# When the operands of the seven products are made in a hybrid decoder layer, and where the second pass's operands and the raw weights stand

## The chip, the cores and the metric

One core of a Trainium2 chip runs the whole layer as one program. The metric is the device time of one execution in microseconds (us), the median of several runs. TensorE (PE in the profile) multiplies into PSUM. VectorE (DVE) and ScalarE (ACT) prepare its operands and empty PSUM. GpSimd (POOL) and SyncE (SP) here mostly issue transfers, each on a queue of its own that goes in order.

## What is computed

A layer runs over 1024 prompt tokens and 8 single decode tokens (T = 1032 columns), all in float32 accuracy. The part that the change touches is the end of the layer: the output projection with its residual, the second norm, and the MLP.

```python
mix = jnp.concatenate([pool_out, rwkv_out], axis=-1) @ w_out     # 1024 x 1024
x = x + mix
h2 = _rmsnorm(x, norm2_g)
x = x + jnp.square(jax.nn.relu(h2 @ w_up)) @ w_down              # 1024 x 4096, 4096 x 1024
y = _rmsnorm(x, norm_f_g)
```

## The kernel before, in words

**Split operands.** Every operand of a large product is split in two parts: a high part `h`, rounded by ACT (`act`, line 94), and a low part `l`, the rest, subtracted by DVE. A product is then three matmuls (h·h, h·l, l·h) for each 128 rows of the contraction (`gemm`, line 185). Weights come from DRAM 128 x 512 at a time. `weights` (lines 159 and 167) and `split` (line 176) put the parts into two rings, `wh` and `wl`, of six tiles each.

**Two passes over the tokens.** Tokens are in channel-major tiles, and everything from the output projection on goes in two halves: 512 columns, then 520 (512 prompt tokens and the 8 decode tokens). `x1[half]` holds the residual stream of a half and is loaded by `load_x1` (line 866).

**Output projection of the second half** (pool `opb`). `mixed` (lines 879 and 881) loads and splits the eight mixer rows. `out_block` (line 885 on) makes one output tile: 21 matmuls of 260 columns into one of two PSUM banks, then one DVE add into `x1` (line 890). Eight output tiles `m`, two column blocks each, take the first seven mixer rows; a second loop of 16 short blocks of 3 matmuls (weights `w7`) adds the eighth row.

**Second norm.** `norm2` squares the residual on ACT, sums over the tiles on DVE (line 921), sums over the partitions by a matmul with ones (line 922), and takes the inverse root (`rstd`, lines 137 to 139).

**The up projection as seven products.** A half's columns are cut in two and the contraction in two, and instead of eight block products seven are made of sums of blocks. `up_operands(half)` makes the seven token operands in high and low parts (names x11, x21, x22, xt1 to xt4, each with h and l), four slices `k` each. A slice `k` takes 15 DVE operations: 4 times norm and gain (line 942), 4 subtractions (line 945), 7 low parts (line 935), and 7 roundings on ACT. `up_pair(p)` makes output tiles 2p and 2p+1: it loads four raw weight blocks a11, a21, a12, a22 on SP's queue (line 974), makes four sums s1 to s4 on DVE in tiles of their own (named `as` in the profile, line 978), splits seven weights, and runs seven products of 12 matmuls (line 991). The outputs are combined (line 1006), squared, and split (line 1002). All raw weights and sums stand in pool `mp`, which is opened after `opb` is closed and lies in its room.

**The down projection.** `downs(G, ms)` yields eight steps for each group `G` of four up tiles: one weight split, 12 matmuls of 512 columns in the first half (24 of 260 in the second), and one or two DVE adds into `x1` (line 1054). `up_pair` takes four such steps between its own products. `G` runs from 0 to 14; pairs 0 to 15 belong to the first half, 16 to 31 to the second, and `G == 7` is the turn: `up_operands(1)` stands there, with four of the eight down steps behind it.

**What sets the order.** The program is written in one order, and a scheduler at compile time puts each engine's instructions into a fixed sequence: of those that it reckons ready, the one written first. On the chip each engine keeps to that sequence and waits where an input is late. A tile can be written again only after its last reader, and a tile in reused room waits for the tiles that stood there.

The end of the out projection before reads:

```python
        load_x1(1)
        norm2(0, 512, lambda x: op.tile([P, 512], F32, tag="n2", name=x, bufs=2))
        up_operands(0)
        for m in range(KT):
            w = weights(I["w_out"][m, :, :(KT - 1) * P])
            for o in (0, 260):
                out_block(m, w, ops, 1, o, 260)
```

## Time and profile before

| What | us |
|---|---|
| median of three runs | 1369.51 |
| lowest and highest of the three | 1365.20, 1369.58 |
| the profiled execution's own time | 1369.36 |
| its span (first to last instruction) | 1367.6 |

The profile is of one execution. Times are us from the start of the span. "Busy" is the time in which an engine executes. "PEclk" or "granted clock" is the TensorE clock in that stretch as a share of full speed: 1.00 is the upper of its two levels, 0.50 the lower. A row such as "PE mx <- DVE x" says which engine waited, with which tile, for whom. A number in square brackets at the end of a row is the idle time of the engine before this instruction, and what ended it.

### The profile page before, as it was taken

To read this page: it belongs to the slowest core of one execution; us is meant where nothing else is said; L and a number is where in the kernel's file an instruction comes from. 1 tells how busy PE (TensorE), PEld (TensorE's weight loads), DVE (VectorE), ACT (ScalarE), POOL (GpSimd) and SP (SyncE) were. 2 spreads that over 40 slices of the span, in tenths; PEclk is the share of its full clock that TensorE was granted. 3 is DMA by queue.
4 is the path that set the end of the run, shared out by engine and by line. 5 is a ranking of instruction groups with operands and counts; after the bars stand their busy time and mean duration, and the time that the engine had idled before them with its cause. 6 is when DMAs were issued, how large, how long until landed. Compare 5 with 4: busy or idle time off the path is not lost.

```text
span 1367.6 us, 26992 instructions
## 1 busy us (share of the span) xinstructions
PE 1277.1 (93%) x10228; PEld 1156.3 (85%) x10228; DVE 1060.8 (78%) x2321; ACT 827.3 (60%) x2004; POOL 88.1 (6%) x178
## 2 busy tenths in 40 slices
PE   5999999999999899958899999999799999999996
PEld 5987888798777767857788989989699999999996
DVE  8887676879777665775887777878989778788775
ACT  7667677766877665533655655546566555455552
POOL 4111001210100211110000000000000000000000
PEclk9999999999999999979899999999899999999998
DMA  6222123322312433512233333332234333333321
GB/s 208 95 55 79 42 58 81 114 75 61 73 43 47 130 136 115 186 56 72 86 108 94 108 102 97 102 101 93 71 100 147 101 94 101 99 95 109 93 63 63
DMA packets 109347, 128.27 MB, mean 94 GB/s; under 512 B 54585, under 2 KB 62905, under 8 KB 109209
## 3 DMA queue, kind: packets, MB, share of 16 engines
q1 hardware_dynamic: 97120, 92.22, 23.1%
q0 software_dynamic: 10240, 32.48, 7.2%
q10 hardware_dynamic: 1856, 1.85, 0.4%
q8 instruction: 80, 1.31, 0.4%
q14 instruction: 51, 0.41, 0.1%
HBM read 113.23 MB, written 13.51 MB: 93 GB/s over the span
## 4 chain that ended last, share of the span: by engine, by line
PE 72%; DVE 12%; ACT 10%; DMA 3%; issue 2%; POOL 1%; SPq 0%; DVEq 0%; ACTq 0%; POOLq 0%
PE dn L185 24%; PE b L991 21%; PE pj L185 10%; PE mx L185 6%; ACT SV L94 2%; PE pcs L608 1%; DVE tm L525 1%; PE sc L431 1%; PE pcs L605 1%; ACT TT L94 1%; PE pcs L601 1%; ACT wh L94 1%; DVE x L1060 1%; DMA a<-in_w_up 1%; PE bkt L445 1%
## 5 line engine op out<-in xcount | busy, mean ns | idle before, releaser
L185 PE MATMUL dn<-uh,wh 128*128 128x260 f32 (+1 forms) x736 | 237.8, 324 | 6.0 <-DVE x L1054 5.4
L185 PE MATMUL dn<-uh,wl 128*128 128x260 f32 (+1 forms) x736 | 237.5, 323 | 2.1 <-DVE wl L167 2.1
L185 PE MATMUL dn<-ul,wh 128*128 128x260 f32 (+1 forms) x736 | 237.3, 323 | 0.1
L94 ACT ACTIVATE wh<-wr 128x512 fp32r<-128x512 f32 x230 | 143.2, 623 | 127.5 <-PE b L991 39.0
L185 PE MATMUL pj<-xh,wh 128*128 128x258 f32 (+3 forms) x576 | 172.7, 300 | 13.9 <-ACT wh L94 13.9
L167 DVE TENSOR_TENSOR wl<-wr,wh 128x512 fp32r<-128x512 f32 x230 | 156.0, 682 | 31.6 <-ACT wh L94 22.5
L185 PE MATMUL pj<-xl,wh 128*128 128x258 f32 (+3 forms) x576 | 170.6, 296 | 0.0
L185 PE MATMUL pj<-xh,wl 128*128 128x258 f32 (+3 forms) x576 | 170.4, 296 | 0.1
L185 PEld LDWEIGHTS dn<-uh,wh 128*128 128x128 f32 x736 | 139.0, 189 | 16.1 <-DVE x L1054 6.0
L1054 DVE TENSOR_TENSOR x<-dn,x 128x260 f32<-128x260 f32 (+1 forms) x192 | 98.7, 514 | 68.0 <-PE dn L185 64.8
L185 PEld LDWEIGHTS dn<-uh,wl 128*128 128x128 f32 x736 | 139.0, 189 | 13.9 <-DVE wl L167 2.8
L185 PEld LDWEIGHTS dn<-ul,wh 128*128 128x128 f32 x736 | 139.1, 189 | 9.3 <-DVE ul L1002 0.4
L94 ACT ACTIVATE wh<-as 128x512 fp32r<-128x512 f32 x128 | 80.1, 628 | 76.5 <-PE dn L185 72.7
L185 PEld LDWEIGHTS pj<-xh,wh 128*128 128x128 f32 x576 | 110.3, 192 | 17.7 <-ACT wh L94 13.9
L94 ACT ACTIVATE wh<-a 128x512 fp32r<-128x512 f32 x96 | 60.5, 632 | 104.1 <-PE dn L185 56.0
L185 PEld LDWEIGHTS pj<-xl,wh 128*128 128x128 f32 x576 | 110.4, 192 | 2.3 <-issue 1.9
L185 PEld LDWEIGHTS pj<-xh,wl 128*128 128x128 f32 x576 | 110.1, 191 | 1.8 <-issue 1.0
L176 DVE TENSOR_TENSOR wl<-as,wh 128x512 fp32r<-128x512 f32 x128 | 87.9, 687 | 4.6
L185 PE MATMUL mx<-mh,wh 128*128 128x260 f32 (+1 forms) x192 | 67.2, 352 | 18.6 <-DVE x L890 18.2
L1002 DVE TENSOR_TENSOR ul<-u,uh 128x256 fp32r<-128x256 f32 (+1 forms) x128 | 54.1, 425 | 21.7 <-ACT uh L94 21.5
L176 DVE TENSOR_TENSOR wl<-a,wh 128x512 fp32r<-128x512 f32 x96 | 65.8, 687 | 4.9 <-ACT wh L94 1.0
L94 ACT ACTIVATE c<-c 128x256 f32<-128x256 f32 (+1 forms) x128 | 53.0, 414 | 21.0 <-DVE c L1006 20.9
(380 smaller groups left out, 3453.4 us busy)
## 6 DMA issues: line engine op xcount, KB each, us to landing
wr<-in_w_down SPq DMA_DIRECT2D x128, 256.0 KB, 2.6
a<-in_w_up SPq DMA_DIRECT2D x128, 256.0 KB, 2.6
wr<-in_w_in POOLq DMA_DIRECT2D x72, 256.0 KB, 3.2
wr<-in_w_out POOLq DMA_DIRECT2D x26, 256.0 KB, 3.3
xr<-in_xT SPq DMA_DIRECT2D x16, 256.0 KB, 3.6
mr<-mix SPq DMA_DIRECT2D x8, 260.0 KB, 3.5
x<-in_xT SPq DMA_DIRECT2D x2, 1040.0 KB, 9.6
blk<-AA SPq DMA_DIRECT2D x16, 128.0 KB, 2.7
```

Source lines behind the costliest of these rows:

```text
L94: A.activation(out, in_, func, bias=bias, scale=scale, **k)
L167: V.tensor_tensor(l[:, :w], raw[:, :w], f32(h[:, :w]), op=ALU.subtract)
L176: V.tensor_tensor(l, raw, f32(h), op=ALU.subtract)
L185: PE.matmul(ps, lhs, rhs, start=i == 0, stop=i == n - 1)
L431: PE.matmul(psc[:, c, :], BK[:, c, 2 * h:2 * h + 2, :], AR[:, c, :, h, :], start=True, stop=True)
L445: PE.transpose(pt[:, c, :], BK[:, c, 2 * h:2 * h + 2, :].rearrange("p a t -> p (a t)"), ident)
L525: V.tensor_tensor(pr[:, q], l[:, q].unsqueeze(2).to_broadcast([64, m, m, m]), r[:, q].rearrange("p k j -> p j k").unsqueeze(1).to_broadcas ...
L601: PE.matmul(pq, AR[:, c, 0, :, :], SV[:, c, :, :], start=True, stop=True)
L605: PE.matmul(pa, TT[:, g, :, :], Q, start=True, stop=True)
L991: PE.matmul(ps, lhs[:, c], rhs, start=k == i == 0, stop=k == 3 and i == 2)
L1002: V.tensor_tensor(ul, u, f32(uh), op=ALU.subtract)
L1054: V.tensor_tensor(d, ps[:, :n], d, op=ALU.add)
```

## The change

- The seven token operands of the first half are made one slice `k` at a time, one slice after every second output tile of the out projection, and not in one run ahead of it. The norm of the first half is made in two blocks of 256 columns in other tiles.
- The norm of the second half moves from between `up_pair(0)` and `up_pair(1)` into `G == 1`.
- The operands of the second half are made a slice each in `G == 2` to `5`, in small tiles `xsh`, `xsl` (two of each), and stored to DRAM tiles `XD` from POOL's queue: 56 stores of 128 x 260. At `G == 7`, 14 loads of 128 x 1040 bring them into the tiles of the first half's operands.
- The raw weights stand in pool `hq`, which is opened before `opb`. Of eight tiles five are left: s1, s2 and s4 are written over a21, a11 and a12. The sums are made behind the split of a12. Load order is a11, a21, a22, a12.
- `load_x1` loads in four pieces of two tiles, not in two of four.

```diff
     def load_x1(half):
-        for k in range(0, KT, 4):
-            SY.dma_start(x1[half][:, k:k + 4, :], I["xT"][:, k:k + 4, c0:c0 + n])
+        for k in range(0, KT, 2):
+            SY.dma_start(x1[half][:, k:k + 2, :], I["xT"][:, k:k + 2, c0:c0 + n])
...
+    XD = {i: [dr.tile([P, 4, 260], F32R, name=f"xd{i}{x}") for x in "hl"] for i in KIND}
+
+    def open_operands(half):
+        for i in KIND:
+            XO[half][i] = [hq.tile([P, 4, 260], F32R, tag=f"x{i}{x}", name=f"x{i}{x}{half}") for x in "hl"]
+            if half:
+                for t, d in zip(XO[half][i], XD[i]):
+                    GP.dma_start(t, d)
+
-    def up_operands(half):
+    def up_operands(half, k):
...
+        def put(i, x):
+            if half:
+                h, l = (mp.tile([P, 260], F32R, tag=f"xs{y}", name=f"xs{i}{y}{k}", bufs=2) for y in "hl")
+            else:
+                h, l = (t[:, k, :q] for t in XO[half][i])
             act(h, x)
             V.tensor_tensor(l, x, f32(h), op=ALU.subtract)
+            if half:
+                for t, d in zip((h, l), XD[i]):
+                    GP.dma_start(d[:, k, :], t)
...
-        a = {}
-        for k in range(2):
-            for f in range(2):
-                i = f"{f + 1}{k + 1}"
-                a[i] = mp.tile([P, 512], F32, tag=f"a{i}", name=f"a{i}_{p}")
-                SY.dma_start(a[i], I["w_up"][f0 + f][:, 512 * k:512 * k + 512])
-        for out, x, y, op in (("s3", "11", "21", ALU.subtract), ("s1", "21", "22", ALU.add), ("s2", "s1", "11", ALU.subtract),
-                              ("s4", "12", "s2", ALU.subtract)):
-            a[out] = mp.tile([P, 512], F32, tag=f"a{out}", name=f"a{out}_{p}")
-            V.tensor_tensor(a[out], a[x], a[y], op=op)
+        a, parts = {}, {}
+        raw = lambda i: hq.tile([P, 512], F32, tag=f"a{i}", name=f"a{i}_{p}")
+        for f, k in ((0, 0), (1, 0), (1, 1), (0, 1)):
+            i = f"{f + 1}{k + 1}"
+            a[i] = raw(i)
+            SY.dma_start(a[i], I["w_up"][f0 + f][:, 512 * k:512 * k + 512])
+
+        def parts_of(s):
+
+            def plus(out, x, y, op, at):
+                a[out] = a[at] if at else raw(out)
+                V.tensor_tensor(a[out], a[x], a[y], op=op)
+
+            if s == "12":
+                parts[s] = split(a[s])
+                plus("s3", "11", "21", ALU.subtract, None)
+                plus("s1", "21", "22", ALU.add, "21")
+                plus("s2", "s1", "11", ALU.subtract, "11")
+                plus("s4", "12", "s2", ALU.subtract, "12")
+                return parts[s]
+            return split(a[s])
...
-        norm2(0, 512, lambda x: op.tile([P, 512], F32, tag="n2", name=x, bufs=2))
-        up_operands(0)
+        for c in (0, 256):
+            norm2(c, 256, lambda x: xtmp(x, 260))
+        open_operands(0)
         for m in range(KT):
             w = weights(I["w_out"][m, :, :(KT - 1) * P])
             for o in (0, 260):
                 out_block(m, w, ops, 1, o, 260)
+            if m % 2:
+                up_operands(0, m // 2)
...
     up_pair(0)
-    for c, n in BLK[1:]:
-        norm2(c, n, tmp)
     up_pair(1)
...
     for G in range(15):
         first, rest = downs(G, range(4)), downs(G, range(4, 8))
+        if G == 1:
+            for c, n in BLK[1:]:
+                norm2(c, n, tmp)
+        if 2 <= G < 6:
+            up_operands(1, G - 2)
         if G == 7:
-            up_operands(1)
+            open_operands(1)
             for _ in first:
                 pass
```

## Rows read from the trace of the kernel before

**Rows 1.** The page's busy time by engine: us, share of the span, instructions.
```profile
PE 1277.1 (93%) x10228; PEld 1156.3 (85%) x10228; DVE 1060.8 (78%) x2321; ACT 827.3 (60%) x2004; POOL 88.1 (6%) x178
```

**Rows 2.** The page's 40 slices, busy tenths of PE, and PE's clock.
```profile
PE   5999999999999899958899999999799999999996
...
PEclk9999999999999999979899999999899999999998
```

**Rows 3.** Busy time by engine in six stretches; then clock, DMA share, GB/s.
```profile
563.30:576.60 13.30, 11.27 (x70) 10.11 (x69) 9.12 (x17) 5.99 (x12) 2.15 (x4) 0.87 0.77 270
576.60:627.60 51.00, 35.38 (x273) 35.17 (x272) 32.14 (x83) 16.88 (x38) 3.66 (x6) 0.83 0.17 50
627.60:637.00 9.40, 8.17 (x48) 6.21 (x47) 6.82 (x17) 0.84 (x2) 0.00 (x0) 1.00 0.00 1
637.00:669.00 32.00, 21.66 (x138) 20.04 (x139) 28.01 (x59) 20.35 (x47) 0.00 (x0) 0.87 0.35 112
789.60:831.80 42.20, 42.20 (x266) 37.93 (x265) 32.72 (x60) 23.33 (x48) 0.00 (x0) 1.00 0.32 102
958.00:990.00 32.00, 25.03 (x118) 20.16 (x117) 29.23 (x72) 17.30 (x45) 0.00 (x0) 0.84 0.21 66
```

**Rows 4.** Waits of PE from 560 to 700 us: total, times, longest.
```profile
PE mx L185 <- DVE x L890: 18.2, 6, 15.6
PE b L991 <- ACT wh L94: 4.1, 2, 3.2
PE ss L922 <- DVE acc L921: 3.2, 1, 3.2
```

**Rows 5.** Waits of PE from 950 to 1000 us, same columns.
```profile
PE dn L185 <- DVE x L1054: 4.1, 1, 4.1
PE dn L185 <- DVE wl L167: 2.1, 1, 2.1
```

**Rows 6.** Timeline of PE, late out projection and the first product: start, us, instruction.
```profile
626.68 0.28 PE L185 MATMUL mx<-mh,wh 128*128 128x260 f32 x1
626.80 0.28 PE L185 MATMUL mx<-ml,wh 128*128 128x260 f32 x1
...
639.90 0.39 PE L991 MATMUL b<-x11h,wh 128*128 128x256 f32 x1 [3.17 <-ACT wh L94]
```

**Rows 7.** Timeline of DVE: residual add, first and last of 60 operand operations.
```profile
571.53 0.43 DVE L890 TENSOR_TENSOR x<-mx,x 128x260 f32<-128x260 f32 x1 [3.17 <-DMA x<-in_xT]
...
576.71 1.66 DVE L942 SCALAR_TENSOR_TENSOR b<-x,vec,rs 128x256 f32<-128x256 f32 x4
...
598.54 0.41 DVE L935 TENSOR_TENSOR xt4l<-b,xt4h 128x256 fp32r<-128x256 f32 x1
```

**Rows 8.** Timeline of SP's queue: first loads of raw up weights.
```profile
636.65 31.68 SPq L974 DMA_DIRECT2D a<-in_w_up  x15
```

**Rows 9.** DVE by kind, 789.6 to 831.8 us: count, busy us, mean ns, idle before.
```profile
L1054 DVE TENSOR_TENSOR x<-dn,x 128x512 f32<-128x512 f32 x8 | 5.5, 692 | 5.2 <-PE dn L185 5.1
L167 DVE TENSOR_TENSOR wl<-wr,wh 128x512 fp32r<-128x512 f32 x8 | 5.5, 686 | 0.3
```

**Rows 10.** ACT by kind, same stretch and columns.
```profile
L94 ACT ACTIVATE wh<-as 128x512 fp32r<-128x512 f32 x8 | 5.0, 629 | 4.7 <-PE dn L185 4.7
L94 ACT ACTIVATE wh<-a 128x512 fp32r<-128x512 f32 x6 | 3.8, 632 | 7.7 <-PE dn L185 4.1 <-PE b L991 3.6
```

**Rows 11.** Timeline at the end of a pair: split of s4, later split of a12.
```profile
833.90 0.68 DVE L176 TENSOR_TENSOR wl<-as,wh 128x512 fp32r<-128x512 f32 x1
...
837.26 0.63 ACT L94 ACTIVATE wh<-a 128x512 fp32r<-128x512 f32 x1 [2.04 <-PE dn L185]
```

**Rows 12.** DVE sums of line 921, whole run: count, shortest, median, longest ns.
```profile
L921 DVE TENSOR_TENSOR acc<-acc,sq x21: 419/429/693, 553.8 to 667.9; 128x260 f32<-128x260 f32 x14, 128x512 f32<-128x512 f32 x7
```

**Rows 13.** The page's DMA issues: KB each, median us from issue to landing.
```profile
a<-in_w_up SPq DMA_DIRECT2D x128, 256.0 KB, 2.6
...
mix<-ys POOLq DMA_DIRECT2D x16, 128.0 KB, 2.2
...
out_yT<-x SPq DMA_DIRECT2D x2, 512.0 KB, 3.1
```

**Rows 14.** Landing of the two 1040 KB loads of x1, 560 to 580 us.
```profile
DMA to landing us min/median/max: 8.0/9.6/11.3
```

More of the change, by code (lines that the diff above doesn't have):

```diff
@@ L927, in up_operands, with normed @@
         c0, n = HALF[half]
         q = n // 2
-        for i in KIND:
-            XO[half][i] = [hq.tile([P, 4, 260], F32R, tag=f"x{i}{x}", name=f"x{i}{x}{half}") for x in "hl"]
-        def put(i, k, x):
-            h, l = (t[:, k, :q] for t in XO[half][i])
+        b = {}
+        def normed(i, kk, o):
+            b[i] = xtmp(f"b{i}_{k}_{half}", q)
+            V.scalar_tensor_tensor(b[i], x1s(kk, o, q), col(V_G2, kk), rs2[:, o:o + q], ALU.mult, ALU.mult)
+        def put(i, x):
[3 more added lines that the diff above has]
+                h, l = (t[:, k, :q] for t in XO[half][i])
@@ L934, in put @@
             act(h, x)
             V.tensor_tensor(l, x, f32(h), op=ALU.subtract)
-        for k in range(4):
-            b = {}
-            def normed(i, kk, o):
-                b[i] = xtmp(f"b{i}_{k}_{half}", q)
-                V.scalar_tensor_tensor(b[i], x1s(kk, o, q), col(V_G2, kk), rs2[:, o:o + q], ALU.mult, ALU.mult)
-            def less(i, x, y, out):
-                V.tensor_tensor(b[out], b[x], b[y], op=ALU.subtract)
-                put(i, k, b[out])
-            normed("11", k, c0)
-            put("11", k, b["11"])
-            normed("21", k + 4, c0)
-            put("21", k, b["21"])
-            normed("12", k, c0 + q)
-            less("t1", "12", "11", "11")
-            normed("22", k + 4, c0 + q)
-            put("22", k, b["22"])
-            less("t2", "22", "11", "11")
-            less("t3", "22", "12", "12")
-            less("t4", "21", "11", "21")
+            if half:
+                for t, d in zip((h, l), XD[i]):
+                    GP.dma_start(d[:, k, :], t)
@@ L960, in _build, with less @@
+        def less(i, x, y, out):
+            V.tensor_tensor(b[out], b[x], b[y], op=ALU.subtract)
+            put(i, b[out])
+        normed("11", k, c0)
+        put("11", b["11"])
+        normed("21", k + 4, c0)
+        put("21", b["21"])
+        normed("12", k, c0 + q)
+        less("t1", "12", "11", "11")
+        normed("22", k + 4, c0 + q)
+        put("22", b["22"])
+        less("t2", "22", "11", "11")
+        less("t3", "22", "12", "12")
+        less("t4", "21", "11", "21")
     ups = {}
@@ L985, in product @@
             ps = (ps_u if i % 3 else ps_m).tile([P, 512], F32, tag="u" if i % 3 else "m", name=f"b{i}_{p}")[:, :q]
-            h, l = split(a[s])
+            h, l = parts_of(s)
             for k in range(4):
```

## The prediction

> **What bounds the kernel now.** I read the busy shares first: PE is busy 93% of the span and DVE 78% [rows 1]. So a gain can only come from stretches in which PE stands still or runs at the lower clock, and what matters is who makes it wait there. The 40 slices show where these are: PE's digit falls to 5 and 8 in slices 18 to 20 (581 to 684 us) and to 7 in the slice at 957 to 991 us, and its clock falls with it [rows 2]. Everything from about 690 to 957 us is full. The first slice and the last are not touched by the change. The stretches behind the weak slices are priced next [rows 3], with the waits that end the idle time [rows 4, 5].
>
> How I price a stretch: a matmul of 260 columns follows the next at 0.12 us at full clock [rows 6]. In the steady state PE is busy for all of 42.2 us of two pairs and eight down steps, with 264 matmuls to do: 168 of the pairs and 96 of the down steps, which are twice as wide, so about 0.117 and 0.234 us each [rows 3]. What a stretch takes beyond that is lost.
> - 563.3 to 576.6 us: 70 matmuls, two of them long, are worth some 9.3 us of the 13.3. Lost 4. The first residual add waited 3.17 us for the load of x [rows 7], and the clock was 0.87 on average [rows 3].
> - 576.6 to 627.6 us: 273 matmuls are worth 32.8 us. Lost 18.2. One wait of 15.6 us on the residual add carries it [rows 4]. DVE made 60 operand operations from 576.7 to 599.0 us in one run [rows 7], the add stood behind them in DVE's sequence, and both PSUM banks were full. Lower clock after the gap is the rest.
> - 627.6 to 637 us: 48 matmuls are worth 5.8 us. Lost 3.6; each short block waits for a DVE add.
> - 637 to 669 us: pairs 0 and 1 are worth 168 x 0.117 = 19.7 us, the norm's matmuls and two down matmuls some 2 more. Lost 10.3: 3.2 us for raw weights, whose loads start at 636.65 us, as the last out block ends [rows 6, 8], 3.2 us for the norm's sum [rows 4], and DVE at 28 of 32 us [rows 3].
> - Right behind it, 669 to 674 us still runs at the lower level; I put that at 2.7 by analogy with the stretch before.
> - 958 to 990 us (the turn): 7.0 us idle, 6.2 of it two waits on DVE [rows 5]. A mean clock of 0.84 means that 0.16 x 32 / 0.5 = 10.2 us ran at the lower level, half speed; PE was busy in some 8 of these, so 4 more. Lost 10.9.
> Together 49.7 us. That is the most that the change can give.
>
> **Out projection and first operands.** Alternation moves 60 DVE operations (22.3 us from 576.7 to 599.0, two residual adds among them [rows 7]) from ahead of six output tiles to between them. No work goes away. From 576.6 to the end of the short blocks PE has 32.8 + 5.8 = 38.6 us of work and DVE 32.1 + 6.8 = 38.9 us [rows 3]: equal. The norm in two blocks adds about an us on DVE (14 sums at about 0.43 for 7 at 0.69 [rows 12]). In place of 60.4 us both together cannot take less than 39; the other end is half of the gain. A slice (5.4 us of DVE) stands ahead of the next tile's adds while one tile's block takes PE 2.5 us and there are two banks, so PE stands a little at each slice. I take 42 us: a gain of 18.4, with ends 10 and 21.5.
>
> **x in four pieces.** The first add needs two tiles of eight. The two loads of 1040 KB landed 8.0 and 11.3 us after issue [rows 14], one behind the other, so a first piece of half the size should come 2 to 3 us earlier and clear most of the 3.17 us wait [rows 7]. Ends 0 and 4 with the clock; I take 2. The Trainium skill, page "DMA: Bandwidth & Descriptors", section "Rules for kernel authors", asks for a MiB or more a transfer, and its section "Anatomy of one DMA" has a fixed 2.0 us for each; by that, an estimate, four pieces cost 12.9 us in a row where two cost 8.9, and the first comes only 1.2 us earlier. The trace differs: the first of the two landed after 8.0 us [rows 14] where the page gives 4.4, with 270 GB/s moving in this stretch [rows 3]; by the page this term would be about 1, not 2.
>
> **Raw weights in their own room, norm moved.** The loads no longer wait for the out projection's room, so the 3.2 us at 639.9 us go [rows 6]; w7's two splits leave ring tiles free, so the first products' weights can be split beside the short blocks. The norm of the second half and its 3.2 us wait leave this place. What is late next is DVE: two pairs without down steps take it 32.7 less 16 operations of down steps (each 0.69 long, 0.6 apart, 9.6 us) = 23.1 us [rows 3, 9], more than PE's 19.7. So I take 24 in place of 32.3: gain 8.3, ends 5 and 10.3. PE then stays nearly busy and the 2.7 us of lower clock behind it mostly go: 2, ends 0 and 2.7.
>
> **The turn.** 22 us of DVE leave it. In their place stand 14 loads of 532 KB. Each waits for the last product of the first half that reads its tile; products of pair 15 free them one by one over its 21 us, and behind it four down steps (11 us) and pair 16's own products stand. A 512 KB transfer took 3.1 us [rows 13]; 14 at this are 43 us in a row, against some 53 us of cover, and they overlap. If POOL's order (x11, xt2, x21, ...) differs from the order of release, only the last, x22 and xt4, come after pair 15, and they are used late. Gain 10, ends 5 and 10.9.
>
> **What it costs.** DVE has 9.5 us free in 42.2 [rows 3]. The norm in G = 1 is 14 sums and 6 more, about 0.34 apart: 6.8 us. A slice in G = 2 to 5 is 5.4. Both fit, at 94% and 90%. Each slice's 14 stores go out on POOL, which has nothing else there. With two tiles for each part, the third rounding waits for the first store: 2.2 us for 128 KB [rows 13] and the issue. ACT and DVE stand in order, so the splits of the next weights queue behind that wait; PE has up to six split tiles ahead. I take 2 us in all, ends 0 and 8. Raw weights: a12 can be loaded again only after the split of s4, done at 834.6 us in a typical pair, while the next pair's a12 is split at 837.3 [rows 11]; 2.7 us for a load of 2.6 [rows 13] and its issue, for which I estimate 0.7. So it is late by about 0.6 us a pair. But that split itself waited 2.04 us for PE to free a ring tile [rows 11], as splits do in general here (13 us of ACT's idle time in 42 [rows 10]). PE's lead hides it: 0, ends 0 and 18 (30 pairs x 0.6).
>
> **The sum.** 18.4 + 2 + 8.3 + 2 + 10 - 2 = 38.7. The profiled execution took 1369.4, as the median of the runs did within 0.2, with 1.8 around the span that stay. 1369.4 - 38.7 = 1331. With all upper ends 49.5: 1320. With the lower ends of the gains (20) and the 8 us of stores: 1357.
>
> **Rivals.**
> - DVE becomes the bound: its sequence is nearly full in the out projection and in G = 1 to 5, and waits that the compiler reckoned shorter break the overlap. Then the out projection gives 10, the pairs 5, the turn 8, and G = 1 to 5 cost 3: gain 20, 1349. For it speaks the equality of 38.6 and 38.9; against it, that DVE work has PE's 9.5 us of slack in each steady group. Chance 0.2.
> - Slower than before: the raw weights. If splits do not run ahead of PE any more, every pair waits for a12: load and issue 3.3 us, less the split before it, about 2 us or more, in 30 pairs, 60 us: 1331 + 60 = 1391. It decides from 1.3 us a pair (38.7 / 30), when the lead of six tiles is gone for good. Against it: ACT's idle time in the steady state ends by PE [rows 10]. Chance 0.06.
> - No change: the gaps only move, because the pairs and the turn are then short of something else (the reloads, at the 43 us in a row, start only behind pair 15 and leave PE 20 us idle, and the out projection gives 20): about 1369. Chance 0.03.
> - Better than the sum: the upper ends, 1318 to 1322. Chance 0.06.
>
> **How the numbers follow.** The forecast has 0.65, with 1322 to 1342 as its own range. To leave out no more than 0.2 the range goes from 1320 to 1354: it takes in DVE as the bound, and leaves out the slower and unchanged cases and thin ends. A change within 0.3% (4 us) is about what a measurement cannot tell from none. Faster 0.91, same 0.03, slower 0.06.
>
> **What would show it.** Right: from 572 to 615 us DVE over 90% busy with operand and add rows mixed, no wait of PE on the residual add over 3 us, the first product of pair 0 at 612 to 619 us with raw loads before 610, a first down step at about 637, clock 1.00 there; at the turn no PE wait over 1 us and x11 loads landing before pair 15 ends. Wrong: waits of PE for `wh` in every pair behind loads of a12, waits of ACT for `xsh` that PE feels, or PE still idle for 10 us in one place.

## The result, and the profile of the changed kernel

The changed kernel took 1336.84 us (median of 4 runs, 1334.8 to 1337.91) beside 1367.62 us for the kernel before on the same chip (4 runs). The ratio is 0.9774, 95% interval 0.9749 to 0.9799. The forecast was 1331; the time lies 6 us above it and in the range. The gain is 30.8 us by the medians and 33.6 by the two profiles, where 38.7 was reckoned. The profiled execution took 1335.81 us, with a span of 1334.0.

The clearest account of where the gain stands comes from one instruction that every pair has: ScalarE's copy of the first product, `p<-b`. The timeline of ScalarE (start, us, instruction) has it for pairs 5, 15 and 16 in the kernel before:

```profile
741.62 0.37 ACT L94 ACTIVATE p<-b 128x256 f32<-128x256 f32 x1
...
952.15 0.36 ACT L94 ACTIVATE p<-b 128x256 f32<-128x256 f32 x1
995.06 0.37 ACT L94 ACTIVATE p<-b 128x260 f32<-128x260 f32 x1
```

and in the changed kernel:

```profile
710.18 0.37 ACT L94 ACTIVATE p<-b 128x256 f32<-128x256 f32 x1
...
922.36 0.36 ACT L94 ACTIVATE p<-b 128x256 f32<-128x256 f32 x1
961.63 0.37 ACT L94 ACTIVATE p<-b 128x260 f32<-128x260 f32 x1
```

Before minus after is 31.4 us at pair 5, 29.8 at pair 15 and 33.4 at pair 16; it is still 33.4 at pair 31, and the spans differ by 33.6. So all that stands ahead of pair 5 gave 31.4 (the out projection, the first pairs, and the second half's norm, whose last matmul comes at 699.1 us), the slices and stores from G = 2 to 5 took 1.6 back, and the turn gave 3.6. I call these three differences the account; the same three are used for each experiment below. Seven of the profiles below (the changed kernel, no reload, half the reload, two raw sets, turn undone, own raw set, three tiles early) have the changed kernel's out projection. Their gain at pair 5 goes from 28.7 to 31.6, which is how far the account of one profile can be trusted.

The stretches that answer to [rows 3] (busy time by engine in each window; then PE's clock, DMA share, GB/s):

```profile
565.00:580.00 15.00, 9.49 (x53) 7.01 (x53) 11.62 (x25) 10.94 (x26) 1.08 (x2) 1.00 0.84 269
580.00:612.00 32.00, 32.00 (x268) 31.94 (x267) 30.69 (x83) 17.05 (x40) 4.20 (x7) 1.00 0.24 74
612.00:625.00 13.00, 11.90 (x96) 11.35 (x95) 12.16 (x28) 3.15 (x6) 0.00 (x0) 1.00 0.30 90
625.00:650.00 25.00, 24.57 (x192) 23.39 (x192) 24.32 (x53) 19.94 (x50) 0.00 (x0) 1.00 0.25 81
925.00:960.00 35.00, 30.51 (x151) 25.09 (x150) 18.95 (x36) 13.04 (x26) 5.29 (x10) 0.90 0.84 280
```

From 580 to 650 us PE is nearly full, at a granted clock of 1.00, and DVE is busy for 96% of 580 to 612, where the kernel before lost most [rows 2, 3]. Two weak places are left: 565 to 580 (5.5 us idle) and the turn, 925 to 960 (4.5 us idle and a clock of 0.90). The waits of PE from 560 to 700 us (total, times, longest) answer to [rows 4]; the 18.2 us on the residual add are 1.4:

```profile
PE ss L922 <- DVE acc L921: 2.4, 2, 1.8
PE mx L185 <- ACT mh L94: 1.9, 2, 1.1
PE mx L185 <- DVE x L890: 1.4, 2, 1.1
```

Those from 915 to 975 us answer to [rows 5]:

```profile
PE dn L185 <- DVE x L1080: 2.7, 2, 2.0
PE dn L185 <- ACT uh L94: 1.8, 1, 1.8
```

What DVE does just before the first of these stands in its timeline:

```profile
926.30 0.68 DVE L167 TENSOR_TENSOR wl<-wr,wh 128x512 fp32r<-128x512 f32 x1
931.55 0.69 DVE L991 TENSOR_TENSOR as<-a,a 128x512 f32<-128x512 f32 x1 [4.57 <-issue]
...
933.10 0.68 DVE L1080 TENSOR_TENSOR x<-dn,x 128x512 f32<-128x512 f32 x1
933.70 0.68 DVE L176 TENSOR_TENSOR wl<-a,wh 128x512 fp32r<-128x512 f32 x1
939.41 0.69 DVE L991 TENSOR_TENSOR a<-a,a 128x512 f32<-128x512 f32 x1 [5.03 <-DMA a<-in_w_up]
...
940.95 0.68 DVE L1080 TENSOR_TENSOR x<-dn,x 128x512 f32<-128x512 f32 x1
```

DVE stands still twice, 4.6 and 5.0 us, ahead of sums of pair 16's raw weights. The view names no releaser for the first of these gaps, but the landing times do: a raw load issued at 924.17 landed at 931.47, just ahead of the sum at 931.55, and one issued at 933.21 landed at 939.31, ahead of the sum at 939.41. The residual adds (L1080) that free PE's PSUM banks come behind them in its sequence. The raw weights themselves are late: their four loads of 256 KB from 915 to 955 us landed after 2.4, 7.3, 6.1 and 5.5 us, in order of issue (only the first went out ahead of the reload), where 2.6 is their median over the whole run, as it was before [rows 13]. In the same stretch POOL issues the reload, 14 transfers of 520 KB:

```profile
921.61 0.53 POOL L932 DMA_DIRECT2D x11l<-xd11l  x1 [127.69 <-PE b L1014]
...
942.44 0.55 POOL L932 DMA_DIRECT2D xt4h<-xdt4h  x1
```

### The profile page after: what moved, and what is told of

Same layout as the page of the kernel before. It is cut to its first block, busy times and chain, and to the rows that moved or that the text cites. A ratio compares the mean times of both kernels' runs of the same rounds, so it can differ in the third digit from the quotient of the medians.

```text
span 1334.0 us, 27179 instructions
## 1 busy us (share of the span) xinstructions
PE 1267.3 (95%) x10230; PEld 1146.4 (86%) x10230; DVE 1050.9 (79%) x2331; ACT 822.5 (62%) x2015; POOL 125.4 (9%) x248
## 4 chain that ended last, share of the span: by engine, by line
PE 68%; ACT 12%; DVE 11%; DMA 5%; issue 4%; POOL 1%; SPq 0%; DVEq 0%; ACTq 0%; POOLq 0%
PE dn L185 23%; PE b L1014 21%; PE pj L185 8%; PE mx L185 4%; ACT SV L94 2%; DMA a<-in_w_up 2%; PE pcs L608 1%; PE sc L431 1%; ACT wh L94 1%; ACT TT L94 1%; PE pcs L605 1%; DVE tm L525 1%; PE pcs L601 1%; DVE wl L167 1%; PE bkt L445 1%
## 5 line engine op out<-in xcount | busy, mean ns | idle before, releaser
L94 ACT ACTIVATE wh<-a 128x512 fp32r<-128x512 f32 x192 | 120.8, 629 | 161.3 <-PE dn L185 85.0
L176 DVE TENSOR_TENSOR wl<-a,wh 128x512 fp32r<-128x512 f32 x192 | 131.3, 684 | 6.2 <-ACT wh L94 3.6
L1080 DVE TENSOR_TENSOR x<-dn,x 128x260 f32<-128x260 f32 (+1 forms) x192 | 97.6, 511 | 41.5 <-PE dn L185 39.9
L991 DVE TENSOR_TENSOR a<-a,a 128x512 f32<-128x512 f32 x96 | 66.2, 689 | 19.0 <-DMA a<-in_w_up 17.5
L1025 DVE TENSOR_TENSOR ul<-u,uh 128x256 fp32r<-128x256 f32 (+1 forms) x128 | 53.6, 423 | 18.8 <-ACT uh L94 18.4
L185 PE MATMUL mx<-ml,wh 128*128 128x260 f32 (+1 forms) x192 | 63.6, 332 | 0.9 <-DVE ml L881 0.9
```

The costliest lines, as they stand in the source:

```text
L94: A.activation(out, in_, func, bias=bias, scale=scale, **k)
L176: V.tensor_tensor(l, raw, f32(h), op=ALU.subtract)
L185: PE.matmul(ps, lhs, rhs, start=i == 0, stop=i == n - 1)
L991: V.tensor_tensor(a[out], a[x], a[y], op=op)
L1025: V.tensor_tensor(ul, u, f32(uh), op=ALU.subtract)
L1080: V.tensor_tensor(d, ps[:, :n], d, op=ALU.add)
```

## The experiments

All are compared with the kernel before on the same chip; its median went from 1366.77 to 1368.05 us from chip to chip, so the difference of two medians in the table can be off by an us for that alone. Ratios with their intervals stand in the table. The last three columns are the account: the gain on the kernel before at pair 5, what is added up to pair 15, and what is added from there to pair 16, in us, from one profile each.

| kernel | us | ratio (95%) | at pair 5 | slices, to pair 15 | turn |
|---|---|---|---|---|---|
| changed | 1336.84 | 0.9774 (0.9749 to 0.9799) | 31.4 | -1.6 | +3.6 |
| no reload | 1329.92 | 0.9731 (0.9714 to 0.9747) | 31.6 | -2.8 | +11.0 |
| half the reload | 1332.44 | 0.9750 (0.9734 to 0.9765) | 30.4 | -3.2 | +10.5 |
| two raw sets, alternating | 1335.33 | 0.9763 (0.9745 to 0.9780) | 28.7 | +0.6 | +3.0 |
| turn undone | 1338.99 | 0.9792 (0.9777 to 0.9807) | 30.7 | +0.2 | +0.6 |
| alternation alone | 1353.67 | 0.9908 (0.9876 to 0.9941) | 15.2 | 0 | +0.9 |
| raw room alone | 1374.81 | 1.0051 (1.0031 to 1.0071) | -7.3 | -0.2 | -0.3 |
| x in two pieces | 1341.90 | 0.9809 (0.9784 to 0.9834) | 25.7 | -2.6 | +5.4 |
| raw weights put back | 1341.45 | 0.9807 (0.9789 to 0.9824) | 23.8 | -3.8 | +6.5 |
| x pieces on POOL | 1340.36 | 0.9799 (0.9784 to 0.9814) | 24.8 | -2.9 | +8.7 |
| next pairs' own raw set | 1331.37 | 0.9735 (0.9714 to 0.9755) | 29.3 | -3.4 | +11.6 |
| three tiles early | 1340.77 | 0.9802 (0.9786 to 0.9819) | 29.6 | -9.2 | +8.3 |
| other room and own raw set | 1328.08 | 0.9719 (0.9700 to 0.9738) | 33.9 | -3.3 | +10.9 |

**The reload taken away.** The second half's operands are still made and stored, but the products read the first half's tiles.

```diff
 def open_operands(half):
+    if half:
+        XO[1] = XO[0]
+        return
...
-            if half:
-                for t, d in zip(XO[half][i], XD[i]):
-                    GP.dma_start(t, d)
+            for t in XO[half][i]:
+                act(t[:, :, 256:260], cst[:, 0:16].rearrange("p (k t) -> p k t", k=4))
```

The last two lines fill four columns that the first half doesn't write and the second half's products read.

> Leaves out: the 14 loads at the turn; the second half's products read the first half's operands, so the second half's outputs are not the reference's. The 56 stores stay. Changed kernel: 1336.8 us; at the turn (pair 15 to pair 16) it gained 3.6 of the 10 us forecast. Theory reload: the 7.4 MB of loads fill the DMA engines from 921 to 949 us, raw up weights land after 5.8 in place of 2.6 us, and the sums that wait for them stand on DVE ahead of the residual adds: without the loads the turn gains 10, so about 1330 us, and no PE wait over 1 us there. Rival raw tiles: the loads of raw weights come too late by themselves because each tile has a single set and sums overwrite it: the turn stays at 3.6, about 1336 us.

It took 1329.92 us, and the turn gave 11.0. PE is full from 915 to 960 us (busy time in a window, columns as above):

```profile
915.00:960.00 45.00, 45.00 (x265) 39.37 (x264) 32.37 (x61) 25.32 (x53) 0.00 (x0) 1.00 0.34 100
```

The same window of the changed kernel:

```profile
915.00:960.00 45.00, 40.51 (x218) 34.26 (x217) 26.34 (x52) 20.47 (x43) 7.42 (x14) 0.92 0.76 251
```

So nothing else of the change holds the turn back when the reload's traffic is gone.

**Half of it.** Only the seven high tiles are reloaded; the low ones stay the first half's.

```diff
...
+                XO[1][i] = [hq.tile([P, 4, 260], F32R, tag=f"x{i}h", name=f"x{i}h1"), XO[0][i][1]]
+                GP.dma_start(XO[1][i][0], XD[i][0])
...
-                for t, d in zip(XO[half][i], XD[i]):
-                    GP.dma_start(t, d)
...
```

> Leaves out: the seven loads of low parts at the turn; the second half's products read the first half's low parts, so its outputs are not the reference's. Half the bytes (3.7 MB) in the same 21 us, about 175 GB/s beside some 100 for weights. Theory reload, by saturation: the engines are no longer full, raw weights land near 3 us, nearly all of the lost 6 us come back: about 1331 us. If the loss goes with the bytes: half of it, about 1333.5 us. Rival raw tiles: no change, about 1336 us.

The turn gave 10.5, nearly all. The window from 915 to 960 us again:

```profile
915.00:960.00 45.00, 44.16 (x261) 38.59 (x261) 31.93 (x61) 24.84 (x52) 3.73 (x7) 1.00 0.57 176
```

By the account the loss is not in proportion to the bytes: 0.5 us beside the run without a reload, where the whole reload lost 7.4. The medians leave that open: of the 6.9 us between the changed kernel and no reload 2.5 are left here, and the time lies between the two answers that were expected, 1331 and 1333.5. The three raw loads of pair 16 that were issued during this reload landed after 4.3, 3.5 and 5.0 us, in place of 7.3, 6.1 and 5.5.

**Two sets of raw tiles, by turns.** Even pairs use one set, odd pairs the other.

```diff
-raw = lambda i: hq.tile([P, 512], F32, tag=f"a{i}", name=f"a{i}_{p}")
+raw = lambda i: (mp if p % 2 else hq).tile([P, 512], F32, tag=f"a{i}", name=f"a{i}_{p}")
```

> Odd pairs' raw weights stand in a second set of five tiles in the free room of the MLP pool, so a raw load can be issued a pair (21 us) ahead; the reload stays whole. Theory raw tiles: raw loads are out before the reload begins, the turn gains its 10 us: about 1330 us. Theory reload alone (bandwidth for everything, down weights too): down weights and raw weights are late all the same, about 1336 us. If both are needed (short lead and full engines), this gives the 6 us back as well as leaving out the loads does.

The turn gave 3.0. This doesn't show that the raw weights are innocent. SP's fixed sequence moved every pair's loads one pair ahead, and DVE's moved the sums as well: pair 16's loads came in time, issued at 898 to 910 us, but pair 17's took their old place in the reload (two at 933.28), and pair 17's first sums stood ahead of the same residual adds. DVE's waits from 915 to 965 us:

```profile
DVE a L991 <- DMA a<-in_w_up: 4.6, 1, 4.6
DVE as L991 <- DMA a<-in_w_up: 4.4, 1, 4.4
```

So the run left the question open, and it told what a better one must do: load no raw weights at all during the reload.

**The turn undone.** The second half's operands are made at the turn, as before, and nothing goes through DRAM.

```diff
...
-        if 2 <= G < 6:
-            up_operands(1, G - 2)
         if G == 7:
             open_operands(1)
+            for k in range(4):
+                up_operands(1, k)
```

> Undoes the DRAM part alone: the second half's operands are made in one run at the turn again, no stores, no loads; all else as in the changed kernel. By what the two traces show (turn +3.6 us, slices in G = 2 to 5 cost 1.6): slower by 2, about 1339 us. By the prediction's terms (10 and 2): slower by 8, about 1345 us. If the turn's loss comes from raw tiles with one set, it is worse here than in the kernel before: over 1347 us.

1338.99 us: the turn gave 0.6, and without slices nothing is lost up to pair 15 (+0.2). The way through DRAM is worth some 2 us as the change has it (2.2 by the medians; by the account 3.6 less 1.6, beside 0.8 here), where 8 were forecast. The intervals of the two ratios overlap, so that it is worth anything at all is not clear of the noise; that it is worth far less than 8 is. That single raw tiles alone hold the turn back (over 1347) fell.

**Alternation alone.** The kernel before, with the norm in two blocks and a fourth of the operands behind every second output tile.

```diff
...
-        norm2(0, 512, lambda x: op.tile([P, 512], F32, tag="n2", name=x, bufs=2))
-        up_operands(0)
+        for c in (0, 256):
+            norm2(c, 256, lambda x: xtmp(x, 260))
+        open_operands(0)
...
                 out_block(m, w, ops, 1, o, 260)
+            if m % 2:
+                up_operands(0, (m // 2,))
...
```

> The kernel before with one part of the change: the norm in two blocks of 256 and the first half's operands made a fourth at a time between the output tiles of the out projection; x still in two pieces, raw weights still in the pool that opens behind the projection, the second half's operands still made at the turn. Theory (the parts add up as in the prediction): 18 to 20 us of the 1367 go, so 1347 to 1349, and pair 15 to 16 shows no gain of its own. Rival (the parts need each other: without early raw weights the first product has nothing to start with): the gain is at most 12, 1355 or more. Rival (the parts of the change at the start are worth all of the 33 us by this one alone): 1338.

1353.67 us: 14.4 us came by the medians and 12.6 by the ratio, 15.2 at pair 5, so less than the 18 to 20 and a little more than the first rival's 12. The out projection itself is repaired, but then PE waits for raw weights, whose loads go out from 621.42 us on: in the second window below (columns as above) it is busy for 8.27 of 13 us.

```profile
580.00:612.00 32.00, 30.61 (x250) 29.89 (x248) 29.37 (x79) 14.21 (x35) 3.67 (x6) 1.00 0.20 62
612.00:625.00 13.00, 8.27 (x47) 6.39 (x48) 8.74 (x22) 2.56 (x6) 0.00 (x0) 0.93 0.30 90
```

**Raw weights' room alone.** The kernel before, with raw weights and sums in room that is open early, and the change's load order and sums in place (`parts_of`).

```diff
...
-                a[i] = mp.tile([P, 512], F32, tag=f"a{i}", name=f"a{i}_{p}")
...
+        raw = lambda i: hq.tile([P, 512], F32, tag=f"a{i}", name=f"a{i}_{p}")
...
```

> The kernel before with one part alone: raw weights in room that is open during the out projection, two of the sums in place, loads in the new order. Theory: the first product of pair 0 waits for its operands anyhow, so little comes of early raw weights alone: 0 to 5 us, 1362 to 1367, with the rest of their price (8 us) to be had only beside the alternation. Rival of the prediction (the tile that is read last, 12, is held until the fourth sum, and the next pair's load starts late): each pair loses, 1375 to 1391.

This part alone makes the kernel 0.5% slower, where the theory had 0 to 5 us of gain. The rival's reason is not it: nothing is lost between pair 5 (-7.3) and pair 31 (-7.5). The loss stands at the start of the second half's out projection, where PE is busy for 9.51 us, at a clock of 0.78, and waits for the mixes' high parts 7.1 us in all. The window:

```profile
565.00:580.00 15.00, 9.51 (x39) 7.63 (x38) 10.24 (x17) 8.92 (x16) 1.33 (x3) 0.78 0.83 266
```

It is the place in which the changed kernel is weak too.

**x in two pieces.** The changed kernel with two loads for each half again, of 1040 KB in the second.

```diff
-        for k in range(0, KT, 2):
-            SY.dma_start(x1[half][:, k:k + 2, :], I["xT"][:, k:k + 2, c0:c0 + n])
+        for k in range(0, KT, 4):
+            SY.dma_start(x1[half][:, k:k + 4, :], I["xT"][:, k:k + 4, c0:c0 + n])
```

> The changed kernel with x of the second half loaded in two pieces of 1040 KB again. Theory (the prediction's term of 2 us): 1338 to 1340. Rival (the four pieces stand in SP's queue ahead of the last loads of the mixes, and the 6 us that the matmul engine idles at 565 to 580 come from that): 1331 to 1334, with the matmul engine busy over 12 of the 15 us from 565 to 580.

1341.90 us, and 25.7 instead of 31.4 at pair 5, below all seven profiles named above: the four pieces are worth some 5 us (the ratios' intervals overlap). The rival fell. In SP's queue (start, us over which the run of instructions was issued) the second large piece goes out at 573.24 and the mixes' seventh load, which the first output tile needs, at 577.47; with four pieces this load goes out at 573.68.

```profile
573.24 0.46 SPq L866 DMA_DIRECT2D x<-in_xT  x1
577.47 0.93 SPq L879 DMA_DIRECT2D mr<-mix  x2
```

The large piece is not what holds this load. It waits for its tile, which is free when DVE has made the fourth low part, and six of the norm's sums stand ahead of that in DVE's sequence:

```profile
573.77 3.06 DVE L921 TENSOR_TENSOR acc<-acc,sq 128x256 f32<-128x256 f32 x6
576.75 1.30 DVE L881 TENSOR_TENSOR ml<-mr,mh 128x520 fp32r<-128x520 f32 x2
```

In the changed kernel it comes between these sums:

```profile
572.96 0.69 DVE L881 TENSOR_TENSOR ml<-mr,mh 128x520 fp32r<-128x520 f32 x1
```

Why the scheduler orders DVE otherwise when x comes in two pieces was not settled.

**Raw weights put back.** The changed kernel with raw weights and sums in the pool behind the out projection, in the old order.

```diff
...
-        raw = lambda i: hq.tile([P, 512], F32, tag=f"a{i}", name=f"a{i}_{p}")
...
+                a[i] = mp.tile([P, 512], F32, tag=f"a{i}", name=f"a{i}_{p}")
...
```

> The changed kernel with the raw weights and their sums back in the pool that opens behind the out projection, in the old load order. Theory (room for raw weights is worth 5 to 8 us at the first product of pair 0): 1342 to 1345. Rival A (the raw loads issued ahead of the mixes' loads delay the second half of the out projection, 6 us at 565 to 580, which pays back what they bring): 1335 to 1338, with the matmul engine busy over 12 of the 15 us from 565 to 580 and a wait of 5 us or more ahead of pair 0. Rival B (single raw tiles also hold back the turn): the turn, pair 15 to 16, gives 8 to 10 us instead of 3.6.

1341.45 us, a little under the theory's range and over rival A's. Both sides of rival A are there all the same: PE has 13.34 us of work at 565 to 580, and a gap of 3.5 us ahead of pair 0 takes some of it back. The windows:

```profile
565.00:580.00 15.00, 13.34 (x100) 12.51 (x99) 11.47 (x27) 9.32 (x24) 2.69 (x5) 1.00 0.72 240
...
612.00:625.00 13.00, 9.53 (x60) 7.66 (x59) 9.03 (x23) 1.68 (x4) 0.00 (x0) 1.00 0.20 56
```

Net, the room and the load order that goes with it are worth 4.6 us here by the medians. They cost some 4 us of work at 565 to 580 that the prediction didn't see. The turn gave 6.5, between the two answers of rival B.

**x pieces from POOL.** I took this loss for SP's order: one x piece waits 8.5 us for the first half's last matmul, with five of the mixes' loads behind it.

```diff
-            SY.dma_start(x1[half][:, k:k + 2, :], I["xT"][:, k:k + 2, c0:c0 + n])
+            (GP if half else SY).dma_start(x1[half][:, k:k + 2, :], I["xT"][:, k:k + 2, c0:c0 + n])
```

> The changed kernel with one thing else: the four x pieces of the second half are issued by POOL, behind its weight loads, instead of by SP. Theory (in the changed kernel the first x piece stands in SP's queue behind the third of the mixes' eight loads, waits 8.5 us for the first half's last matmul, and the mixes' loads 4 to 8 wait behind it, which costs the 5 to 6 us of idle matmul engine at 565 to 580): 1330 to 1333, with 85 or more matmuls at 565 to 580 instead of 53, all eight mix loads issued before 566, and the gain up to pair 5 at 36 to 37 us instead of 31. Rival (the raw loads ahead of the mixes' loads, or the traffic of the four x pieces, cost this time): 1335 to 1338, with the matmul engine still idle 5 us.

This theory fell: 1340.36 us, over the rival's range too, and 37 matmuls at 565 to 580. With x out of its way SP still took 22.81 us over the mixes' loads (SP's timeline):

```profile
557.00 22.81 SPq L879 DMA_DIRECT2D mr<-mix  x8
```

The pieces now go out in one run, at 566.99 to 569.12, and the mixes' next three loads beside them landed after 5.2 to 5.8 us, where they took 2.6 to 2.9 in the changed kernel. All eight go through three tiles; a tile is free when ScalarE has split it and DVE has made the low part from that. ScalarE's timeline shows what stands in its sequence, here in the changed kernel:

```profile
567.67 0.47 ACT L94 ACTIVATE ms<-ss,sm 128x256 f32<-128x256 f32 x1 [1.37 <-PE ss L922]
568.04 0.63 ACT L94 ACTIVATE mh<-mr 128x520 fp32r<-128x520 f32 x1
```

and here with the raw weights put back:

```profile
557.87 2.03 ACT L94 ACTIVATE mh<-mr 128x520 fp32r<-128x520 f32 x3
...
570.52 0.48 ACT L94 ACTIVATE ms<-ss,sm 128x256 f32<-128x256 f32 x1 [1.15 <-PE ss L922]
```

Where the raw weights have the early room, the first split of a mix comes at 566.6 to 569.9 us (ten kernels: the changed one, no reload, half the reload, two raw sets, turn undone, raw room alone, x in two pieces, x pieces on POOL, own raw set, three tiles early), behind squares of the norm that need the first half's last output tile. Where the mixes' tiles have their old place, it comes at 555.5 to 557.9 (the kernel before, alternation alone, raw weights put back). ScalarE keeps to its sequence, so PE stands.

This run shows one thing more. From 667 us on it has the changed kernel's instructions, in the same sequence on every engine, and yet its turn gave 8.7 where the changed kernel's profile gave 3.6. The three raw loads of pair 16 that were issued during its reload landed after 6.8, 2.9 and 6.0 us, where the changed kernel's took 7.3, 6.1 and 5.5, and PE idled 2.7. What the reload costs differs from one profile to the next; the account's 3.6 is one draw of it, and the run with x in two pieces (5.4), which has that sequence too, another.

**A set of their own for pairs 16 and up.** Pair 16's raw weights come before the reload and pair 17's behind it.

```diff
-raw = lambda i: hq.tile([P, 512], F32, tag=f"a{i}", name=f"a{i}_{p}")
+raw = lambda i: (mp if p > 15 and i != "s3" else hq).tile([P, 512], F32, tag=f"a{i}", name=f"a{i}_{p}")
```

> The changed kernel with the raw weights of pairs 16 and up in a second set of four tiles, so that pair 16's are loaded before the reload begins and pair 17's after it. Theory (the turn is lost because VectorE, in order, waits some 9 us for pair 16's slowed raw weights ahead of residual adds that the matmul engine needs): the turn, pair 15 to 16, gives 8 to 10 us instead of 3.6, 1330 to 1333, with no wait of VectorE on raw weights from 920 to 960. Rival (the rate itself: weights of the down projection and the operands land late just the same): the turn gives 3 to 5, 1335 to 1338, with matmul idle of 4 us or more at 925 to 960 behind other names.

1331.37 us, the turn gave 11.6, with the whole reload and nearly the same traffic, in the window from 915 to 960 us:

```profile
915.00:960.00 45.00, 45.00 (x266) 39.42 (x265) 33.81 (x63) 24.67 (x52) 7.43 (x14) 1.00 0.72 236
```

The weights of the down projection still landed late, 5.4 us at the median, and PE doesn't feel it. The rate by itself is not what stops PE; it is the raw weights, through DVE's order. PE's, ScalarE's and POOL's sequences are the changed kernel's from end to end; besides SP's loads only twelve of DVE's instructions, from 922 to 939 us, stand in another order. This profile is of the longest of its four runs (1333.48), is 2.1 us behind the changed kernel's at pair 5 and loses 1.8 more up to pair 15, so its span is only 2.3 us shorter; the 5.5 us are the difference of the medians, and the intervals of the two ratios just meet.

**Three tiles early.** Three of the fourteen get room of their own, so that eleven are reloaded at the turn.

```diff
+    EARLY = ("11h", "11l", "t2h")
...
-            XO[half][i] = [hq.tile([P, 4, 260], F32R, tag=f"x{i}{x}", name=f"x{i}{x}{half}") for x in "hl"]
+            XO[half][i] = [mp.tile([P, 4, 260], F32R, tag=f"y{i}{x}", name=f"y{i}{x}") if half and i + x in EARLY else
+                           hq.tile([P, 4, 260], F32R, tag=f"x{i}{x}", name=f"x{i}{x}{half}") for x in "hl"]
```

> The changed kernel with three of the fourteen operand tiles of the second half (11 high and low, t2 high) in room of their own, loaded before pair 15, so that eleven are reloaded at the turn. Theory (the stall goes with the reload's bytes: with seven tiles the turn gave 10.5 us, with fourteen 3 to 4): 5 to 8 us at the turn, 1332 to 1335. Rival (any reload beyond some size costs the same): 3 to 4, 1336 to 1338.

The turn gave 8.3, at the upper end of the theory's 5 to 8, but the run with x pieces on POOL gave as much with fourteen, so this doesn't show that the loss goes with the bytes. The kernel took 1340.77 us: the three early loads go out at 779.29, 784.41 and 792.65 us, among the slices' stores, and between pairs 5 and 15 9.2 us are lost instead of 1.6. A row of ScalarE's waits from 770 to 860 us, here and then in the changed kernel:

```profile
ACT wh L94 <- DMA a<-in_w_up: 7.0, 2, 6.5
...
ACT wh L94 <- DMA a<-in_w_up: 8.3, 3, 3.4
```

and one of PE's from 770 to 850 us, which the changed kernel doesn't have:

```profile
PE dn L185 <- ACT uh L94: 4.2, 2, 3.5
```

In all ScalarE waits no longer here, but once for 6.5 us, and PE then waits behind it. The early loads and the stores together make raw weights late here too; how much of the 9.2 each has was not told apart.

**Both places mended.** The set of their own for pairs 16 and up, and the first set in the room of the first half's mixes, on the other side of the memory. The second half's mixes keep their old place.

```diff
 open_x1(1)
+rp = open_pool(ctx, "raws", side="right", reuse_waits="tile")
...
-raw = lambda i: hq.tile([P, 512], F32, tag=f"a{i}", name=f"a{i}_{p}")
+raw = lambda i: (mp if p > 15 and i != "s3" else rp).tile([P, 512], F32, tag=f"a{i}", name=f"a{i}_{p}")
```

> The changed kernel with the second set of the run before (pairs 16 and up) and with the first set of raw weights in other room: that of the first half's operands of the out projection, free when the first half ends, so that the tiles of the second half's mixes keep the places that they have in the kernel before. Theory (the 5 to 6 us of idle matmul engine at 565 to 580 come from ScalarE's order, in which the mixes' splits stand behind the norm's squares and its mean once the raw weights' room has shifted the mixes' tiles; with the old places they stand ahead): 1324 to 1328, with 85 or more matmuls at 565 to 580 instead of 53, no wait ahead of pair 0, and 34 to 38 us gained on the kernel before up to pair 5, the turn keeping its 11. Rival (the raw loads, now later, collide with the x pieces and land after pair 0 could start, as where the raw weights were put back): 1330 to 1334, with idle of 3 us or more at 612 to 625.

1328.08 us, ratio 0.9719 (0.9700 to 0.9738): the best kernel here, its interval below the changed one's. Time and gain at pair 5 (33.9) lie just outside what the theory gave; its signs are there. ScalarE's timeline has the mixes' splits ahead of the norm again:

```profile
556.11 0.62 ACT L94 ACTIVATE mh<-mr 128x520 fp32r<-128x520 f32 x1
...
568.83 0.48 ACT L94 ACTIVATE ms<-ss,sm 128x256 f32<-128x256 f32 x1 [1.15 <-PE ss L923]
```

The four windows of the start, columns as above:

```profile
565.00:580.00 15.00, 13.21 (x103) 12.54 (x102) 11.52 (x29) 8.73 (x23) 2.15 (x4) 1.00 0.89 306
580.00:612.00 32.00, 30.43 (x246) 29.45 (x245) 30.11 (x82) 15.20 (x37) 3.12 (x5) 1.00 0.20 65
612.00:625.00 13.00, 13.00 (x110) 12.81 (x109) 12.80 (x30) 5.50 (x12) 0.00 (x0) 1.00 0.39 123
625.00:650.00 25.00, 23.19 (x157) 21.42 (x156) 22.66 (x46) 17.57 (x42) 0.00 (x0) 0.93 0.36 116
```

103 matmuls stand where the changed kernel has 53, and no gap opens ahead of pair 0. At pair 0 the gain on the kernel before is 22.4 us, where the changed kernel has 16.0; at pair 5 it is 33.9, beside 31.4 in the changed kernel and 29.3 in the run that differs from this one by the room alone. The difference goes into DVE, which is at 91 to 98% from 580 to 650, and into the lower clock at 625 to 650. By the medians the room is worth 3 us, with intervals that overlap; the rows leave no doubt that ScalarE's order and the idle time at 565 to 580 go with it.

## Why the prediction was nearly right, step by step

**The bound.** Right: all of the gain came from the weak slices of [rows 2], and little changed behind the turn (a gain of 33.2 at pair 17 and 33.4 at pair 31).

**Out projection, x, raw weights, clock.** The four terms made 30.7 us up to the steady groups; 31.4 came. (24 us in place of the 32.0 of [rows 3] is 8.0, not the 8.3 of the third term; it changes nothing.) The sum was right and its parts were not, so that it came this near is in part luck: x brought more than was put for it, and a loss at 565 to 580 was not priced at all. Alternation alone gave 15.2 at pair 5 (term 18.4, ends 10 and 21.5). The raw room alone gave -7.3 (term 8.3 with the norm, ends 5 and 10.3), and within the changed kernel +7.6 at pair 5 and +4.6 in the medians; the norm's move was not run by itself. The missed step was in "the loads no longer wait for the out projection's room": new room moves every tile behind it, the scheduler then put the mixes' splits behind the norm in ScalarE's sequence, and 5.5 us of idle PE at 565 to 580 (1.7 with the raw weights put back) paid part of the gain back. What stands against it is the stretch behind, full from 580 to 612 at a clock of 1.00. Why the other room makes the scheduler reckon so was not settled; the runs show only that the two go together.

**x in four pieces.** Right in sign and too small: 2 forecast with ends 0 and 4; the run with two pieces lost 5.1 us by its median and 5.7 at pair 5, against a spread of some 3 in the account. The reason was not the one forecast. No residual add waits for x in either profile, and the first piece landed after 4.3 us where the larger one took 5.6, so 1.3 sooner and not 2 to 3. With two pieces the mixes' seventh load goes out 3.8 us later, behind DVE's sums. The Trainium skill, "DMA: Bandwidth & Descriptors", section "Rules for kernel authors", asks for a MiB or more a transfer; by it the pieces of 520 KB should have been the worse ones. The measurement decides here: the kernel with the smaller ones was some 5 us faster, with an order of DVE that came with them; what of it the size of the pieces brings by itself was not tried. The section "Anatomy of one DMA" of that page of the Trainium skill, from which the prediction has a fixed 2.0 us, is on transfers that GpSimd issues; here SyncE issues x.

**The turn.** This is the term that was mis-sized: 10 forecast with ends 5 and 10.9, 3.6 in the profiled execution. The miss is some 6 us (1336.84 for 1331), and the medians say the same as the account: the changed kernel became 5.5 us faster when only the raw weights of pairs 16 and up were moved out of the reload's time, and 6.9 when the reload was left out. The step that failed is the price put on the reload, "14 at this are 43 us in a row, against some 53 us of cover, and they overlap". As far as it goes it came true: the reload was in time, issued at 921.6 to 942.4, landing after 3.7 to 9.0 us, the first tile well before pair 15's end. But it prices the reload by its own deadline alone and puts at nothing what it does to the loads beside it. Raw weights issued during it landed after 5.5 to 7.3 us in place of 2.6, down weights after 5.8 at the median, DVE waited 9.6 us for the raw ones in front of residual adds, PE idled 4.5 and its clock was 0.90. The rate alone is not the cause: with own raw tiles the whole reload ran, the down weights were nearly as late (5.4), and the turn gave 11.6.

**The costs.** Slices and stores: 2 forecast (0 to 8), 1.6 measured, 2.6 to 3.8 in seven other profiles with the same stores. With the raw weights a pair ahead they cost nothing (the run with two sets by turns, +0.6), which speaks for late raw weights as their way too; it was not tried by itself. The reuse of single raw tiles was put at 0, and it is 0 in the steady state: the gain doesn't shrink from pair 17 to pair 31. At the turn it is not: single raw tiles without a reload gave 11.0 there, a reload with a set of their own for pairs 16 and up 11.6, and the two together 3.6 to 8.7.

**The rivals.** DVE as the bound (1349): not in the main, though DVE is at 96% in the out projection. Slower by the raw tiles (1391): the raw room alone was slower, but at the mixes and by 7 us in one place, not by 2 in each pair. No change: no. Better than the sum: no.

**What would show it.** The signs that came as forecast: DVE busy for 40.56 of 43 us (94%) from 572 to 615, no wait on the residual add over 1.1 us, the first product of pair 0 at 615.20, its raw loads issued by 555.2, clock 1.00. Not as forecast: the first down step came at 645.02 (664.38 in the kernel before) and not at about 637, since a part of pair 2 now goes ahead of it; and at the turn two waits of PE were 2.0 and 1.8 us, not under 1. That is the sign that named the miss.

## What to carry to other kernels

Price a new transfer twice: by its own deadline, and by what its rate does to the loads that run beside it, with the in-order engine that waits for these. When a bulk transfer can't be spread, move the small loads that an engine waits for out of its time; here that made the kernel 5.5 us faster with the same bytes. New room for one set of tiles moves others and so the fixed sequence: read the order of each engine in the trace of the changed kernel before trusting a sum of parts.

## What the runs showed of the hardware

A load of 256 KB landed after 2.6 us in the steady state (102 GB/s in [rows 3]). The raw loads of pair 16 that were issued during the reload landed after 7.3, 6.1 and 5.5 us in the changed kernel (251 GB/s from 915 to 960) and after 4.3, 3.5 and 5.0 with half the reload (176 GB/s). The rate alone doesn't set the time: with x pieces on POOL (260 GB/s) they took 6.8, 2.9 and 6.0. The loads were SP's and the traffic beside them POOL's, so another engine's queue was no shelter; the Trainium skill, page "DMA: Bandwidth & Descriptors", section "Issuing engines are not separate DMA queues", says so (they run on the same DMA engines and interleave), and the trace agrees. By the turn's gain beside the run without a reload (11.0), seven transfers of 520 KB cost 0.5 us and fourteen 2.3, 5.6 and 7.4, in three profiles with the same sequence; how the cost grows between seven and fourteen the runs don't settle.
